# A two-layer hybrid transformer block: group C first in the mixer, and the projections of the conv, D and A beside later attention

## Chip, core and metric

One core of a Trainium2 chip. The metric is the device time of one execution in microseconds (us); the kernel before was executed three times, and once more with a profile.

## What is computed

The block has two layers. Each modulates and normalizes 512 latent tokens (and 256 context tokens) of width 1024, projects them once by `w_in` and cuts the result into four head groups. Cut to what the change touches:

```python
def hybrid_mixer(hx, hc, ...):
    qa, ka, va, ub, qc, kc, vc, qd, kd, vd = project(hx, w_in)        # and the same of hc
    y_a = window_gqa(qa, ka, va, ka_c, va_c, sink)                    # A: windowed attention
    y_b = conformer_conv(ub, conv_w, conv_b, conv_ln_g, conv_ln_b)    # B: 31 taps, depthwise
    y_c = diff_out(diff_attention_latent(qc, kc, vc, kc_c, vc_c, lam), subln_g, lambda_init)
    y_d = neighbourhood_attn(qd, kd, vd, kd_c, vd_c, rpb)             # D: 2-D windows
    return concatenate([y_a, y_b, y_c, y_d]) @ w_out                  # layer 0 also for the context
def diff_weights(q, k, v, lam):                                       # C: two softmaxes per head
    p = softmax(einsum(q, k) * C_QK_DIM ** -0.5)
    return einsum(p[:, :, 0] - lam * p[:, :, 1], v)
```

A gated residual, a SwiGLU network of hidden width 2816 and a second gated residual follow. The last layer drops the context's outputs.

## The kernel before

All tensors are kept in float32 accuracy: each weight and each activation is split into a high part and a low part (`split`, L138: a cast on ScalarE, then a subtraction, L143, on VectorE or GpSimd), and `mm3` (L173) multiplies high by high, high by low and low by high. A "unit" is 128 output columns of `w_in`: 24 matmuls of 512 latent columns, and 24 of 256 context columns where the context is needed, into a PSUM pair. It is loaded by SyncE's queue, split, multiplied and taken out of PSUM.

The mixer of a layer is written as Python generators, which `layer` (L985) interleaves: `beside` (L918) runs a main generator and advances a side one at a ratio, `mix2` (L937) alternates two, `take` and `chain` cut and join them. This written order is the input of a list scheduler with a timeline, which then fixes the order of the instructions of each engine; what an engine does at a given place is therefore read from the built order and not from the Python code.

Before, the mixer starts with three units of the conv (`first_units`, L441, with the columns `B0`, whose weights `ahead_b` asked for), which fill the time while the activations are still being normalized. `proj_b` (L568) makes the conv's gated input `hp` (L587) from two units for each half u. `conv_taps` (L862) is 29 multiply-adds (L873) on VectorE for each half, after the first tap on ScalarE (L870), and L877 for the last. `proj_c` (L552) makes q and k of a half of C and, for half 0, V. Then come `c_attn` (L632) for halves 0 and 1, `d_attn` (L772) for halves 0 and 1 and `a_attn` (L820), each beside projections of the next group: C's half 0 beside the rest of C's projections and D's half 0, C's half 1 beside the rest of D, D beside A. In C a step is a score of two softmaxes (L625), two maxima with the weighted copy out of PSUM (L656), exponentials on ScalarE, and one multiply-add on VectorE (L665), on which TensorE's transposes (L510) and the product with V (L616) wait. In D the score is L788, the maximum L799 and the division L816 on GpSimd. In A they are L625, L849 and L816; its context queries go through L729 to L743. The norms of C and of the conv (`c_norm`, L673, `conv_norm`, L881) stand beside D's half 1. `load_wo` (L947) splits the output projection's weights.

## Time and profile before

| | us |
|---|---|
| three executions | 1812.6, 1810.37, 1809.29 |
| median | 1810.37 |
| profiled execution | 1809.8 |
| span of its profile | 1808.0 |
| mixer of layer 0, start of the first units to w_out | 58 to 427 |
| mixer of layer 1 | 1085 to 1380 |

The profile is of one execution. A row of the page's first part gives an engine's busy time, its share of the span and its count of instructions. In a window's row the first number after the stretch is its length, then follow busy times by engine, the clock that TensorE was granted (1.00 is the full one) and the share and rate of the DMA. In a timeline's row the bracket at the end holds the engine's idle time ahead of the instruction and what ended it. Outside the two mixers TensorE has hardly any gap.

### The profile page before, as it was taken

How to read it: one execution, taken by the hardware profiler on the slowest of the kernel's cores; microseconds unless marked ns; L12 is line 12 of the kernel's file. 1: busy time of each engine (PE TensorE's matmuls, PEld its weight loads, DVE VectorE, ACT ScalarE, POOL GpSimd, SP SyncE). 2: the span in 40 equal slices, each digit the busy share in tenths (PEclk: the TensorE clock that was granted, in tenths of full speed). 3: DMA queues.
4: the chain of work that ended last, by engine and by line, in shares of the span. 5: the costliest groups of instructions: out<-in, count | busy, mean ns of one | idle time of the engine just before them, and what ended most of it. 6: DMA issues, size and time to landing. Idle time of an engine off the chain costs nothing.

```text
span 1808.0 us, 26990 instructions
## 1 busy us (share of the span) xinstructions
PE 1715.8 (95%) x11236; PEld 1415.6 (78%) x11236; DVE 941.5 (52%) x1546; ACT 586.3 (32%) x1052; POOL 216.8 (12%) x200
## 2 busy tenths in 40 slices
PE   6898999888999999999999999999988999999997
PEld 4786787666898878888888888878766888888886
DVE  5599656664362442332424347976565445444354
ACT  4223553553151112121120224345355332321322
POOL 1101202340000010000100011130342000000002
PEclk8998999898999999999999999999999999999999
DMA  9351102215134344234231221120225173323321
GB/s 322 89 155 36 45 24 78 82 38 201 60 93 143 121 140 130 83 96 131 62 107 43 83 81 59 49 66 25 89 61 175 36 209 93 105 83 92 117 70 47
DMA packets 187977, 172.79 MB, mean 96 GB/s; under 512 B 17878, under 2 KB 150478, under 8 KB 187726
## 3 DMA queue, kind: packets, MB, share of 16 engines
q1 hardware_dynamic: 187854, 171.06, 31.0%
q8 instruction: 88, 1.44, 0.3%
q14 instruction: 35, 0.29, 0.0%
HBM read 166.76 MB, written 4.52 MB: 95 GB/s over the span
## 4 chain that ended last, share of the span: by engine, by line
PE 81%; DVE 9%; DMA 4%; ACT 2%; issue 2%; POOL 1%; SPq 1%; POOLq 0%; ACTq 0%; DVEq 0%
PE ps L176 19%; PE ps L177 19%; PE ps L178 19%; PE pu L176 4%; PE pu L178 4%; PE pu L177 4%; DVE accd L873 3%; PE pt L616 2%; PE sc L625 2%; PE pt L510 2%; PE ada L306 2%; PE pu L616 1%; DVE Pm L656 1%; SPq L97 1%; DMA araw<-in_w_ada 1%
## 5 line engine op out<-in xcount | busy, mean ns | idle before, releaser
L177 PE MATMUL ps<-h,whi 128*128 128x512 f32 (+1 forms) x1104 | 383.5, 348 | 2.5 <-DVE h L143 2.5
L176 PE MATMUL ps<-h,whi 128*128 128x512 f32 (+1 forms) x1104 | 382.5, 349 | 0.9 <-DVE gt L974 0.9
L178 PE MATMUL ps<-h,wlo 128*128 128x512 f32 (+1 forms) x1104 | 382.9, 347 | 0.0
L141 ACT CAST whi<-wraw 128x1024 fp32r<-128x1024 f32 (+1 forms) x132 | 134.5, 1023 | 445.7 <-PE ps L177 246.8
L143 DVE TENSOR_TENSOR wlo<-wraw,whi 128x1024 fp32r<-128x1024 f32 (+1 forms) x116 | 140.1, 1211 | 199.0 <-ACT whi L141 198.0
L177 PEld LDWEIGHTS ps<-h,whi 128*128 128x128 f32 x1104 | 209.0, 189 | 29.8 <-DVE h L143 3.2
L176 PEld LDWEIGHTS ps<-h,whi 128*128 128x128 f32 x1104 | 207.8, 189 | 29.7 <-issue 2.8
L178 PEld LDWEIGHTS ps<-h,wlo 128*128 128x128 f32 x1104 | 208.8, 189 | 27.5 <-issue 2.0
L176 PE MATMUL ps<-wdhi,zh 128*128 128x512 f32 x440 | 171.7, 392 | 0.4 <-ACT ntmp L381 0.4
L177 PE MATMUL ps<-wdlo,zh 128*128 128x512 f32 x440 | 171.0, 390 | 0.0
L178 PE MATMUL ps<-wdhi,zl 128*128 128x512 f32 x440 | 170.5, 391 | 0.0
L176 PE MATMUL pu<-hT,whi 128*128 128x512 f32 (+1 forms) x456 | 163.2, 358 | 4.8 <-DVE hp L587 2.2
L177 PE MATMUL pu<-hT,whi 128*128 128x512 f32 (+1 forms) x456 | 160.7, 353 | 0.0
L178 PE MATMUL pu<-hT,wlo 128*128 128x512 f32 (+1 forms) x456 | 160.5, 352 | 0.0
L974 DVE TENSOR_TENSOR gt<-ps,g 128x1024 f32<-128x1024 f32 x66 | 80.6, 1222 | 142.7 <-PE ps L178 114.3
L141 ACT CAST wdhi<-wraw 128x1024 fp32r<-128x1024 f32 x44 | 46.1, 1052 | 271.3 <-PE ps L178 181.0
L977 POOL TENSOR_TENSOR x<-x,gt 128x1024 f32<-128x1024 f32 x12 | 29.7, 2474 | 729.8 <-DVE gt L974 729.8
L873 DVE SCALAR_TENSOR_TENSOR accd<-hp,wcol,accd 128x783 f32<-128x783 f32 (+1 forms) x116 | 112.8, 972 | 2.8 <-ACT accd L870 1.2
L1241 DVE TENSOR_TENSOR sg<-sg,ps 128x768 f32<-128x768 f32 (+1 forms) x44 | 36.1, 821 | 144.1 <-PE ps L178 116.1
L176 PEld LDWEIGHTS pu<-hT,whi 128*128 128x128 f32 x456 | 86.5, 190 | 21.0 <-issue 2.6
L176 PEld LDWEIGHTS ps<-wdhi,zh 128*128 128x128 f32 x440 | 82.6, 188 | 19.3 <-issue 1.4
L178 PEld LDWEIGHTS pu<-hT,wlo 128*128 128x128 f32 x456 | 86.8, 190 | 12.7 <-issue 1.8
(263 smaller groups left out, 2730.3 us busy)
## 6 DMA issues: line engine op xcount, KB each, us to landing
araw<-in_w_ada SPq DMA_DIRECT2D x60, 512.0 KB
wraw<-in_w_gate SPq DMA_DIRECT2D x44, 512.0 KB
wraw<-in_w_up SPq DMA_DIRECT2D x44, 512.0 KB
wraw<-in_w_down SPq DMA_DIRECT2D x44, 512.0 KB
wraw<-in_w_in SPq DMA_DIRECT2D x40, 512.0 KB
wraw<-in_w_ada SPq DMA_DIRECT2D x20, 512.0 KB
wraw<-in_w_out SPq DMA_DIRECT2D x12, 512.0 KB
whi<-in_w_ada SPq DMA_DIRECT2D x8, 512.0 KB
```

What stands on the lines that cost most here:

```text
L141: nc.scalar.copy(hi, src)
L143: eng.tensor_tensor(lo, src, f32(hi), op=ALU.subtract)
L176: mm(out, st[0], mv[0], start=first, stop=False)
L177: mm(out, st[0], mv[1], start=False, stop=False)
L178: mm(out, st[1], mv[0], start=False, stop=last)
L306: nc.tensor.matmul(ps[32 * j:32 * j + 32, 0:P], self.cstat[:, k, :], raw[:, a * 512 + j * P:a * 512 + (j + 1) * P], start=(k == 0), stop=( ...
L510: self.nc.tensor.transpose(pt[:, (i - a) * P:(i - a + 1) * P], blocks[i], self.ident)
L616: self.burst_of([lambda i=i, j=j: nc.tensor.matmul(po[64 * j:64 * j + 64, 0:P], *parts[j][i], start=(i == n - 1), stop=(i == 0)) for i in ...
L625: return [lambda o=o, q=q[a][r], k=k[b][r], i=i: self.nc.tensor.matmul(o, q, k, start=(i == 0), stop=(i == 2)) for i, (a, b) in enumerate( ...
L873: nc.vector.scalar_tensor_tensor(acc[:, 0:w], hp[:, k:k + w], wc, acc[:, 0:w], op0=ALU.mult, op1=ALU.add)
L974: nc.vector.tensor_tensor(tmp, ps, g, op=ALU.mult)
L1241: nc.vector.tensor_tensor(sg, sg, pss[1][:, 0:W], op=ALU.mult)
```

## The change

The first three units are now C's q and k of half 0 and one unit of the conv (`FIRST`); `first_units` takes a flag for the context for each unit, and `qk_unit` accepts a unit that is already in PSUM. After C's q and k and the conv's half 0 follow V, some taps and the modulation's loads. C's half 0 stands beside the conv's half 1 and the rest of C, C's half 1 beside D's half 0 and D's V, D's half 0 beside D's half 1 and C's norm, D's half 1 beside three units of A, and A beside A's last unit, the conv's norm, the loads of w_out and the modulation. The taps are given to C and D by `spread`. The conv's pool stays until A ends, and there are 9 buffers of the tag "qk" instead of 12. The diff, without the renaming of `ahead_b` and the changes of `first_units`:

```diff
...
-    QKB = 12
+    QKB = 9
...
-        lat, cx = self.unit(u, H, ctx, order)
+        lat, cx = u if len(u[0].shape) == 2 else self.unit(u, H, ctx, order)
...
-            self.qkc[nm, u] = self.qk_unit(self.w_unit(w, c0 + u * P), H, cx, sc, pool, (C_CC, C_SC, 1))
+            got = self.first.pop(c0 + u * P, None)
+            self.qkc[nm, u] = self.qk_unit(got or self.w_unit(w, c0 + u * P), H, cx, sc, pool, (C_CC, C_SC, 1))
...
-    B0 = (UB + 256, UB, UB + 256 + P)
+    FIRST = (CQ, CK, UB + 256)
...
+    def spread(self, main, side, nm, ns):
+
+        k = i = 0
+        for c in main:
+            i += 1
+            while k * nm < ns * i:
+                next(side, None)
+                k += 1
+            yield c
...
-        for u in range(2):
-            for _ in self.mix2(self.proj_b(l, H, c1, u), tp if u else iter(()), 3, False):
-                pass
+        self.half = 0
...
-        for _ in self.mix2(self.mix2(self.proj_c(l, H, c1, 0), tp, 6, False), adas, 2, False):
+        pc = self.proj_c(l, H, c1, 0)
+        for _ in self.mix2(self.take(pc, 2), self.proj_b(l, H, c1, 0), 1):
             pass
-        for _ in adas:
+        for _ in self.mix2(self.mix2(pc, tp, 5, False), adas, 4):
             pass
...
-        self.beside(self.mix2(self.c_attn(l, 0), tp, 1 + l, False),
-                    self.chain(self.proj_c(l, H, c1, 1), self.proj_d(l, H, c1, 0)), 2 * nq, 4)
-        self.beside(self.mix2(self.c_attn(l, 1), tp, 1 + l, False), d_rest(), 2 * nq, 4)
+        self.beside(self.spread(self.c_attn(l, 0), tp, 2 * nq, 14),
+                    self.chain(self.proj_b(l, H, c1, 1), self.proj_c(l, H, c1, 1)), 2 * nq, 4)
+        self.beside(self.spread(self.c_attn(l, 1), tp, 2 * nq, 16), self.chain(self.proj_d(l, H, c1, 0), d_v()), 2 * nq, 4)
         self.psum_pop()
         self.psum_push("e")
+        self.act_evac = False
         dn = 10 if cx else 8
         pa = self.proj_a(l, H, c1)
-        self.beside(self.d_attn(l, held["c2"], 0), self.take(pa, 3), dn, 3)
-        self.beside(self.d_attn(l, held["c2"], 1), rest(), dn, 14 if cx else 9)
+        self.beside(self.spread(self.d_attn(l, held["c2"], 0), tp, dn, 17),
+                    self.chain(self.proj_d(l, H, c1, 1), self.c_norm(l, c1)), dn, 5 if cx else 4)
+        for _ in tp:
+            pass
+        self.beside(self.d_attn(l, held["c2"], 1), self.take(pa, 3), dn, 3)
...
-        self.beside(self.chain(self.a_attn(l, 0), self.a_attn(l, 1)), more(), 2 * dn, 12)
+        self.beside(self.chain(self.a_attn(l, 0), self.a_attn(l, 1)), more(), 2 * dn, 21 if cx else 18)
         wop = held["wop"]
         held["c2"].release()
+        self.cv.release()
...
```

The built order, at the three places that the prediction speaks of. (The diff adds lines, so L656, L665, L873, L877 of before are L657, L666, L874, L878 of the change; `accd` is a tap's sum, `Pm` a softmax's weights, `sc` and `sd` the scores of C and D.)

First, VectorE at the end of layer 0's conv. Before, 30 taps stand ahead of C's first softmax and 28 behind it, and the last ones between the eighth step and the ninth:

```order
L656 ISA Pm_1694,nm_1693<-sc_1679,zcol_92 128x768
L656 ISA nm_1693 128x1
L656 ISA Pm_1698,nm_1697<-sc_1679,zcol_92 128x768
L656 ISA nm_1697 128x1
L873 SCALAR_TENSOR_TENSOR accd_1251<-hp_764,wcol_698,accd_1251 128x783
L143 TENSOR_TENSOR qk_1894<-pu_1895,qk_1893 128x512
L877 SCALAR_TENSOR_TENSOR yB_745<-hp_764,wcol_698,accd_1251 128x512
L877 SCALAR_TENSOR_TENSOR yB_745<-hp_764,wcol_698,accd_1251 128x256
```

With the change 19 stand ahead and 39 behind, and the last ones beside the tenth step, a narrow one of the context:

```order
L666 SCALAR_TENSOR_TENSOR Pm_1690<-Pm_1694,cf_1699,Pm_1690 128x256
L657 ISA Pm_1721,nm_1720<-sc_1708,zcol_92 128x256
L657 ISA nm_1720 128x1
L874 SCALAR_TENSOR_TENSOR accd_2011<-hp_1162,wcol_698,accd_2011 128x783
L663 RECIPROCAL rl_1724<-l_310_1715 128x1
L874 SCALAR_TENSOR_TENSOR accd_2011<-hp_1162,wcol_698,accd_2011 128x783
L665 SCALAR_TENSOR_TENSOR cf_1726<-L_184_1121,nlam_713,rl_1724 128x1
L874 SCALAR_TENSOR_TENSOR accd_2011<-hp_1162,wcol_698,accd_2011 128x783
L666 SCALAR_TENSOR_TENSOR Pm_1717<-Pm_1721,cf_1726,Pm_1717 128x256
L878 SCALAR_TENSOR_TENSOR yB_745<-hp_1162,wcol_698,accd_2011 128x512
L878 SCALAR_TENSOR_TENSOR yB_745<-hp_1162,wcol_698,accd_2011 128x256
```

So the conv ends two steps of C later than before, and ahead of D in both.

Second, TensorE in layer 0's D half 0, with the change: a piece of the run from one unit's last matmul (`pu`) to the next unit, over seven D scores (L789 and L626, of six rows each, two shown):

```order
L178 MATMUL pu_2828<-hT_71_342,wlo_2822 128x256
L510 MATMUL ptd_2771<-ident_88,Pm_2762 128x128 x4
L789 MATMUL sd_2907<-qk_2112,qk_1917 128x256 x2
L789 MATMUL sd_2907<-qk_2113,qk_1917 128x256 x2
...
L685 MATMUL pu_2937<-ident_88,yC_746 128x128 x4
...
L510 MATMUL ptd_2811<-ident_88,Pm_2802 128x128 x4
L789 MATMUL sd_2985<-qk_2112,qk_1917 128x256 x2
```

Between these scores only transposes and products with V stand (L510, L617, L685); four units of A follow in one piece. Before, the units stand between D's scores up to the seventh, and none behind it.

Third, VectorE at the end of layer 0's A. Before, two splits of w_out and three of the next weights (two are in this piece) stand among the rows of the last context softmax (L729 to L743):

```order
L732 TENSOR_SCALAR nm_943_4520<-nm_943_4520,sink_714 128x2
L143 TENSOR_TENSOR wolo_971_4611<-wraw_4608,wohi_970_4610 128x1024
L734 TENSOR_SCALAR es_945_4524<-nm_943_4520,sink_714 128x2
L143 TENSOR_TENSOR wlo_4626<-wraw_4623,whi_4625 128x1024
L524 COPY PT_4486<-pt_4490 128x512
L729 TENSOR_REDUCE nm_949_4541<-sc_4506 128x2
L740 TENSOR_TENSOR ls_944_4522<-ls_944_4522,es_945_4524 128x2
L143 TENSOR_TENSOR wlo_4632<-wraw_4629,whi_4631 128x1024
```

With the change they stand behind it, and six earlier ones at the start of A, which were in D before:

```order
L143 TENSOR_TENSOR wolo_860_4172<-wraw_4168,wohi_859_4171 128x1024
L901 TENSOR_SCALAR qk_3775<-pu_3765,bmv_3770,brs_3772 128x256
L143 TENSOR_TENSOR wolo_869_4195<-wraw_4191,wohi_868_4194 128x1024
L850 ISA Pm_3676,nm_3678<-sc_3663,mask_3657,sink_714 128x512
...
L744 TENSOR_SCALAR Pm_4539<-Pm_4539,ls_950_4542 128x256 x2
L524 COPY PT_4496<-pt_4497 128x512
L143 TENSOR_TENSOR wolo_968_4605<-wraw_4602,wohi_967_4604 128x1024
L143 TENSOR_TENSOR wolo_971_4611<-wraw_4608,wohi_970_4610 128x1024
```

So A's last softmax has no split ahead of it, and A's first (L850) has two.

## Rows read from the trace of the kernel before

**Rows 1.** The page: busy time, share of the span and instructions of TensorE.

```profile
PE 1715.8 (95%) x11236; PEld 1415.6 (78%) x11236; DVE 941.5 (52%) x1546; ACT 586.3 (32%) x1052; POOL 216.8 (12%) x200
```

**Rows 2.** Windows of layer 0: length, busy (instructions) per engine, granted clock, DMA.

```profile
72.00:126.00 54.00, 50.94 (x428) 43.95 (x428) 45.34 (x55) 11.46 (x17) 1.95 (x1) 1.00 0.48 139
126.00:187.00 61.00, 53.24 (x321) 42.41 (x321) 59.16 (x87) 23.86 (x47) 10.33 (x4) 0.89 0.16 45
...
206.50:284.00 77.50, 75.44 (x556) 60.04 (x554) 44.19 (x113) 38.36 (x94) 4.76 (x2) 1.00 0.14 36
...
328.70:358.30 29.60, 22.34 (x181) 16.56 (x180) 21.50 (x51) 19.31 (x43) 12.04 (x9) 0.83 0.40 125
358.30:386.00 27.70, 19.03 (x162) 14.30 (x162) 20.97 (x70) 16.78 (x45) 13.05 (x15) 0.88 0.00 1
...
407.00:427.00 20.00, 12.48 (x102) 8.95 (x103) 11.95 (x25) 11.91 (x33) 2.04 (x2) 0.75 0.51 162
```

**Rows 3.** Windows of layer 1, same columns.

```profile
1148.00:1207.00 59.00, 55.99 (x340) 43.29 (x339) 56.06 (x92) 28.40 (x56) 19.97 (x17) 0.97 0.25 67
...
1267.00:1324.00 57.00, 53.48 (x433) 41.44 (x432) 32.73 (x79) 23.46 (x58) 23.58 (x29) 1.00 0.22 71
1324.00:1380.50 56.50, 45.91 (x509) 34.83 (x507) 35.59 (x103) 34.85 (x78) 21.98 (x22) 0.94 0.30 87
```

**Rows 4.** Timeline at 167 us: start, length, engine, line [idle before <-releaser].

```profile
167.50 3.09 DVE L665 SCALAR_TENSOR_TENSOR Pm<-Pm,cf,Pm 128x768 f32<-128x768 f32 x1
...
170.74 1.51 PE L510 MATMUL pt<-ident,Pm 128*128 128x128 f32 x6 [4.72 <-DVE Pm L665]
```

**Rows 5.** Timeline in D's end, TensorE.

```profile
336.50 0.66 PE L510 MATMUL ptd<-ident,Pm 128*128 128x128 f32 x4 [2.64 <-POOL Pm L816]
```

**Rows 6.** Timeline at A's end, VectorE: one of five weight splits.

```profile
412.34 1.21 DVE L143 TENSOR_TENSOR wolo<-wraw,wohi 128x1024 fp32r<-128x1024 f32 x1
```

**Rows 7.** Timeline at A's end, TensorE.

```profile
419.21 1.09 PE L510 MATMUL pt<-ident,Pm 128*128 128x128 f32 x4 [2.65 <-DVE Pm L743]
```

**Rows 8.** Timeline, TensorE: C's first and twelfth score, D's first.

```profile
125.79 0.97 PE L625 MATMUL sc<-qk,qk 32*128 32x512 f32 x6
...
208.96 0.63 PE L625 MATMUL sc<-qk,qk 32*128 32x256 f32 x6
...
284.14 0.98 PE L788 MATMUL sd<-qk,qk 64*128 64x256 f32 x12 [0.35 <-DVE nm L656]
```

**Rows 9.** Timeline, TensorE: first and last of a unit's 48 matmuls.

```profile
94.96 0.50 PE L176 MATMUL pu<-hT,whi 128*128 128x512 f32 x1
...
103.37 0.28 PE L178 MATMUL pu<-hT,wlo 128*128 128x256 f32 x1
```

**Rows 10.** Groups of VectorE in layer 0's mixer: busy us, mean ns of one.

```profile
L873 DVE SCALAR_TENSOR_TENSOR accd<-hp,wcol,accd 128x783 f32<-128x783 f32 x58 | 63.9, 1102 | 1.8 <-ACT accd L870 1.2
L656 DVE CUSTOM_DVE_ANT_0 Pm<-sc,zcol 128x768 f32<-128x768 f32 x32 | 29.3, 952 | 15.2 <-PE sc L625 15.1
L665 DVE SCALAR_TENSOR_TENSOR Pm<-Pm,cf,Pm 128x768 f32<-128x768 f32 x16 | 18.3, 1145 | 0.3
```

**Rows 11.** Timeline, VectorE: the conv's last operations, layer 0.

```profile
191.34 1.14 DVE L877 SCALAR_TENSOR_TENSOR yB<-hp,wcol,accd 128x512 f32<-128x512 f32 x2
```

**Rows 12.** Timeline, VectorE: taps while GpSimd splits a weight.

```profile
130.66 3.01 DVE L873 SCALAR_TENSOR_TENSOR accd<-hp,wcol,accd 128x783 f32<-128x783 f32 x2
...
137.86 2.55 DVE L873 SCALAR_TENSOR_TENSOR accd<-hp,wcol,accd 128x783 f32<-128x783 f32 x1
```

**Rows 13.** Groups of GpSimd in layer 0's mixer.

```profile
L816 POOL TENSOR_TENSOR Pm<-Pm,r 128x512 f32<-128x512 f32 x24 | 25.5, 1074 | 94.8 <-DVE r L815 93.7 <-PE pt L616 0.8 <-PE pu L178 0.3
L143 POOL TENSOR_TENSOR wlo<-wraw,whi 128x1024 fp32r<-128x1024 f32 x8 | 19.8, 2481 | 148.6 <-ACT whi L141 148.6
```

**Rows 14.** Timeline, TensorE: C's first score in layer 1.

```profile
1147.95 1.32 PE L625 MATMUL sc<-qk,qk 32*128 32x512 f32 x12
```

**Rows 15.** Groups of VectorE in layer 1's mixer.

```profile
L873 DVE SCALAR_TENSOR_TENSOR accd<-hp,wcol,accd 128x512 f32<-128x512 f32 x58 | 48.9, 843 | 1.0
```

More of the change, by code (lines that the diff above doesn't have):

```diff
@@ L447, in first_units @@
                 a = two[n]
-                outs.append((a[:, 0:512], a[:, 512:768] if nctx else None))
+                outs.append((a[:, 0:512], a[:, 512:768] if nctx[n] else None))
             else:
-                outs.append((self.ps("pu"), self.ps("pu")[:, 0:256] if nctx else None))
-        groups = [(0, 0, 256), (0, 256, 512)] if not by_k else [(0, 0, 512)]
-        if nctx:
-            groups.insert(0, (1, CTX0, CTX0 + 256))
-        for g in [groups] if by_k else [[g] for g in groups]:
-            self.abreast(ws, [[o[1] if x else o[0][:, a:b] for x, a, b in g] for o in outs], H, g, by_k)
+                outs.append((self.ps("pu"), self.ps("pu")[:, 0:256] if nctx[n] else None))
+        cgr = (1, CTX0, CTX0 + 256)
+        for g in [[cgr, (0, 0, 512)]] if by_k else [[(0, 0, 256)], [(0, 256, 512)], [cgr]]:
+            on = [n for n in range(len(c0s)) if nctx[n] or not g[0][0]]
+            self.abreast([ws[n] for n in on], [[outs[n][1] if x else outs[n][0][:, a:b] for x, a, b in g] for n in on],
+                         H, g, by_k)
             if between:
@@ L560, in proj_c, with ahead_first @@
             yield from self.v_units(w, CV, H, self.v_to(self.VC))
-    def ahead_b(self, l):
-        for c0 in self.B0:
+    def ahead_first(self, l):
+        for c0 in self.FIRST:
             self.ahead(self.t["w_in"][l], c0)
-    B0 = (UB + 256, UB, UB + 256 + P)
+    FIRST = (CQ, CK, UB + 256)
     def proj_b(self, l, H, pool, u):
@@ L1007, in layer @@
             next(adas)
-            self.ahead_b(0)
+            self.ahead_first(0)
             for _ in adas:
@@ L1047, in layer @@
         self.psum_push("c")
-        self.first_units(l, H, self.B0, cx, l == 0,
+        self.first_units(l, H, self.FIRST, (cx, True, cx), l == 0,
                          l and (lambda: self.norm_pair(1, 0, self.rows, order[0], H, npool, "pt")))
@@ L1071, in layer, with d_v @@
         tp = taps()
-        for u in range(2):
-            for _ in self.mix2(self.proj_b(l, H, c1, u), tp if u else iter(()), 3, False):
-                pass
+        self.half = 0
         self.burst, self.ada_tag, self.atags = 0, "pt", [("wraw", 3, F32, self.wst)]
         adas = self.ada_gen([(0, 3)] if l == 0 else [])
-        for _ in self.mix2(self.mix2(self.proj_c(l, H, c1, 0), tp, 6, False), adas, 2, False):
+        pc = self.proj_c(l, H, c1, 0)
+        for _ in self.mix2(self.take(pc, 2), self.proj_b(l, H, c1, 0), 1):
             pass
-        for _ in adas:
+        for _ in self.mix2(self.mix2(pc, tp, 5, False), adas, 4):
             pass
-        held = {}
         wo, wa = [], (6, 2)[l]
         nq = 6 if cx else 4
-        def d_rest():
-            yield from self.proj_d(l, H, c1, 1)
-            for _ in tp:
-                pass
-            self.cv.release()
-            self.act_evac = False
+        held = {}
+        def d_v():
             c2 = held["c2"] = self.pool("mixd", "left")
@@ L1098, in d_rest, with more @@
                 yield
-        def rest():
+        def more():
             yield from pa
-            self.half = 0
             hTp.release()
             held["wop"] = self.pool("wo", "right")
-            self.maska = self.tl(held["c2"], [P, 768], "mask")
-            self.dma(self.maska[:, 0:640], t["maska"])
-            yield from self.c_norm(l, c1)
             yield from self.conv_norm(l, c1)
-        def more():
             self.burst, self.ada_tag = 15, ("pu", "pt")[l]
@@ L1257, in layer @@
                     pass
-                self.ahead_b(1)
+                self.ahead_first(1)
                 h2p.release()
```

3 lines of the change are left out of this document (2 added, 1 removed).

## The prediction, made before the changed kernel ran

> **What bounds the kernel now.** I read the engine table first: PE is busy 1715.8 of 1808.0 us [rows 1]. Almost all the time is matmul work that the change leaves as it is; what can be won or lost is PE's lost time, which is its idle time and its busy time at a lowered clock. The windows show where that lies [rows 2]. For a window, loss = length − PE busy + (1 − clock) × length; the last term because a granted clock of 0.89 means that 22% of the window ran at half speed (1.2 instead of 2.4 GHz), which costs 11% of it. In layer 0 that gives 3.1 us in 72:126, 14.5 in 126:187 (7.8 idle, 6.7 clock), 2.1 in 206.5:284, 12.3 in 328.7:358.3 (7.3 and 5.0), 12.0 in 358.3:386 and 12.5 in 407:427: 56.5 us. In layer 1 it is 4.8 in 1148:1207, 3.5 in 1267:1324 and 14.0 in 1324:1380.5: 22.3 us [rows 3]. So the change could win at most about 79 us.
>
> Next I asked what ends the losses. In 126:187 DVE is busy 59.16 of 61.0 us [rows 2]: PE waits for DVE there, which has the conv's taps and C's softmax in one queue. The longest gap is 4.72 us, ended by the DVE multiply L665 [rows 4]. In D's end (328.7:358.3) no projection is left to fill PE while it waits for the softmax and for L816 on POOL: one gap is 2.64 us [rows 5]. At the end of A the context softmax stands behind weight splits in DVE's queue [rows 6], and PE waits 2.65 us for L743 [rows 7].
>
> **The change, part by part.** The arithmetic stays the same and only its order changes, so I price each stage by what PE loses in it.
>
> *From the start to C's twelfth score.* The first C score stands at 125.79 us [rows 8]. A unit of 768 columns takes 48 matmuls, the first at 94.96 and the last at 103.37 us: 8.4 us [rows 9], which is 24 of 512 columns at 0.233 and 24 of 256 at 0.117. In the built order six units' worth of matmuls (50.4 us at these prices) stand ahead of the first score where eight stood (67.2). So the score comes 16.8 us earlier, and of the 3.1 us lost ahead of it I take 2 as saved: 107 us.
>
> From there DVE is the limit, and it has more to do than before. 39 of the 58 taps now stand behind the first score on DVE, where 28 did; 19 stand ahead of it, where 30 did. All 58 end before C's eleventh step: none goes to D, whatever the new call of `spread` says. Up to the end of the conv DVE does 39 taps at 1.10 us (43.0), 16 wide L656 at 0.95 (15.2), 8 wide L665 at 1.145 (9.2) [rows 10], and some 63 small operations (narrow steps, reads, factors, two weight splits, rope), which I estimate from the same rows by their widths at 19 in all. Sum 86: the conv would end at 193. The means hold contention with POOL's weight splits already; if four of those cost DVE their share once more (below), it is 199. Before, the conv ended at 192.4 [rows 11], with two units more done. I put the twelfth score at 198 instead of 208.96 [rows 8]; but 16.8 us of projection that were done by then are still to do: 198 + 16.8 = 214.8, some 6 us behind (1 to 10). Part of the gaps takes rope transposes that stood later, so I take **+5**. The cover that kept DVE's taps cheap was PE's own work ahead of C; it is gone, and what is late next is PE itself, behind L666.
>
> A split on POOL lasts 2.48 us [rows 13]. Beside one, a tap took 2.55 (1.10 is the mean of all), two taps 3.01 (for 2.2), an L665 3.09 (for 1.145) [rows 4, 12]: 1.4 us lost on DVE in the mean. The Trainium skill (SBUF — State Buffer, section "SBUF: two separate sides") has a rule that speaks against this change: GpSimd and a DVE operation with two SBUF inputs take a shared port pair by an exclusive lock, and the loser is blocked for the whole of the other's instruction. By that rule a DVE queue packed with taps would pay up to 2.5 for each of some six splits, 6 us more than by the rows, and the sum below would be +9 instead of +3.
>
> *C's second half, up to D's first score*, is bounded by PE: 77.5 us with 2.1 lost [rows 2]. The matmuls between the two scores are the same within about 1 us. **0.**
>
> *D.* Before, 19.6 us of projection (built order, at the prices above) stood in D, and its last 29.6 us had none; now 37.3 us stand in it. But they stand in two pieces: the built order has a run of seven D scores without a unit, then four units. Each of the seven groups needs two L816 on POOL at 1.07 us [rows 13], so 2.1, and on PE a score of 0.98 [rows 8] with transposes and value products of about twice that, so 3: PE can go on if the scores run ahead. The six w_out splits that DVE did in this window (1.21 each [rows 6]) have left D. I take a loss of 7 where 12.3 were, between 4 (a third of it, as if only the half of the idle time stayed) and 9 (seven groups at the old window's share). **−5.**
>
> *A.* It has no unit beside its attention, as before. At its end the last context softmax has no weight split ahead of it on DVE any more: the gap of 2.65 us [rows 7] and most of the lowered clock behind it go, 5 to 8 of the 12.5 lost there. But the six w_out splits (7.3 us on DVE) and the rope of A's last unit now stand among A's first softmaxes, where PE lost 12.0 already, and the conv's norm is there too. They cost between 0 (if DVE's gaps take them) and 10; I take 5. **−1.5**, from −8 to +5.
>
> *Layer 1.* Its unit is 5.6 us (24 × 0.233), so the first C score, at 1147.95 before [rows 14], comes 11 us earlier, at 1137. Then 38 taps stand behind it instead of 27: 38 at 0.84 (32.0 [rows 15]) and seven softmaxes at 3.6 (25, by rows 10 two L656, one L665 and 0.5 of small ones) put DVE's part of the eighth step at 1194 or later; I put that score, at 1207 before, at 1197. By then 14.2 us of projection are still to do that were done before: 4 us behind, and a bit of clock, **+5** (0 to 8). D: seven score groups with less beside them than before, **+2.5**; A: the units that end later cover D's end instead, **−2.6**.
>
> *Edits that cost nothing.* D's bias tiles are built early on POOL, while the first units run; were they to hold the split queued behind them, a unit would wait once, no longer than two splits (5 us). Two more splits of each layer go to POOL and leave DVE. Nine qk buffers instead of twelve hold what lives together in this order; if one is short, one C step waits. The FFN is untouched.
>
> The sum: 5 + 0 − 5 − 1.5 + 5 + 2.5 − 2.6 = +3.4 us. The profiled execution took 1809.8 us, 0.6 under the median of 1810.37, so 1813.2 on the one scale and 1813.8 on the other: I say **1813**. A measurement of this kernel can tell about 0.2%, 3.6 us, from no change; the forecast is inside that.
>
> **The rivals.**
> *Faster: the cover works.* C's scores run far enough ahead of DVE, and PE has units of B, C and D to do meanwhile. C's first stage then loses half of what it did: −7. D loses 2, as its covered part did: −10. A loses 6 less at its end and pays nothing at its start: −6. Layer 1 as forecast: +5. That is −18, 1792. For it: every one of these gaps has its cause in the rows, and the last cause is surely removed. Against: DVE was busy 97% of 126:187 [rows 2] and gets 11 taps more. Chance 0.30.
> *Slower: DVE stays the bound for the whole of C's first half.* PE idles 20 us there and twice falls to the lower clock (4 each): 28 lost where 17.6 were, +10. Layer 1 does the same, +8. In A the six splits hold the first softmaxes and the clock falls once more, +5 after its end's gain. D wins 5. That is +18, 1828. It decides from the point where the conv ends after about 203 us. For it: DVE's 86 us are a sum without a single gap. Chance 0.25.
> *The change does what its words say*, and the taps go on into D. The built order excludes it; DVE would end C's first half some 15 us earlier and the first rival would hold, which its chance includes.
>
> **How the numbers follow.** The forecast has 0.45 (1806 to 1820): of it 0.06 lies below 1806.8, 0.22 within 3.6 us of no change, 0.17 above. With the rivals: faster 0.36, same 0.22, slower 0.42. The range for 8 in 10 reaches into both rivals: 1794 to 1829.
>
> **What would show it.** C's first score at 105 to 109; the end of the conv (L878) at 193 to 199, with DVE over 95% busy between them and PE losing 20 to 24 us; D's first score near 270 instead of 284.14; 4 to 9 us lost in D; A's first score within 4 us of 358; the gap behind L744 at A's end gone, and new gaps behind L850 at its start. A conv that ends before 188, or an A that loses under 18, would make the forecast wrong on the fast side; a conv that ends after 203 on the slow one.

## The result, and the profile after

| | before | with the change |
|---|---|---|
| runs (us) | 1812.6, 1810.37, 1809.29, 1811.31 | 1825.97, 1821.45, 1825.4, 1826.75 |
| median (us) | 1810.84 | 1825.68 |
| ratio, 95% interval | | 1.0077 (1.0059 to 1.0096) |
| span of the profile (us) | 1808.0 | 1824.0 |

The change makes the kernel 0.8% slower, some 14 us by the ratio. The engine row of the page says that TensorE does the same work, 4.5 us more of busy time in 16 us more of span:

```profile
PE 1720.3 (94%) x11236; PEld 1419.1 (78%) x11236; DVE 942.5 (52%) x1537; ACT 584.0 (32%) x1057; POOL 230.4 (13%) x204
```

The places of the loss follow from the starts of the first instruction of each stage in both traces. A stage that is longer because it holds more projection is not slower, so its projection is counted by the prices of the prediction (0.233 and 0.117 us a matmul).

| stage | us before | us after | projection moved out (−) or in (+) | lost (+) or won (−) |
|---|---|---|---|---|
| layer 0, first units to D's first score (from 58) | 226.1 | 217.9 | −17.7 | +9.4 |
| D of layer 0 | 74.1 | 84.5 | +17.7 | −7.3 |
| A of layer 0 | 68.6 | 62.9 | 0 | −5.7 |
| w_out and FFN of layer 0 | 663.9 | 666.5 | 0 | +2.6 |
| layer 1, first units to D's first score | 176.1 | 185.7 | −8.0 | +17.6 |
| D of layer 1 | 57.6 | 64.6 | +8.0 | −0.9 |
| A of layer 1 | 56.1 | 56.1 | 0 | 0 |
| rest | 427.5 | 427.9 | 0 | +0.4 |

The last column sums to 16 us, the difference of the spans. So C's stage lost 27 us in both layers together, D and A won 14, and 2.6 were lost behind A. The windows of layer 0 (columns as in [rows 2], which they answer to):

```profile
96.00:103.20 7.20, 0.24 (x3) 0.03 (x1) 1.27 (x2) 0.00 (x0) 0.00 (x0) 0.79 0.54 152
...
140.00:170.00 30.00, 29.30 (x220) 24.81 (x221) 28.99 (x47) 12.65 (x26) 5.07 (x2) 1.00 0.12 36
170.00:187.90 17.90, 16.16 (x111) 13.14 (x109) 17.83 (x26) 7.39 (x18) 2.50 (x1) 0.90 0.11 30
187.90:204.00 16.10, 9.03 (x66) 5.98 (x66) 16.07 (x34) 8.13 (x25) 2.36 (x1) 0.79 0.11 33
...
275.90:312.00 36.10, 31.30 (x298) 24.53 (x298) 28.36 (x76) 19.39 (x54) 21.95 (x27) 1.00 0.04 11
312.00:347.00 35.00, 34.15 (x234) 28.29 (x232) 10.40 (x22) 7.48 (x19) 4.76 (x5) 1.00 0.21 62
...
360.30:386.00 25.70, 17.77 (x143) 12.98 (x141) 23.19 (x62) 15.88 (x35) 12.50 (x12) 0.80 0.48 143
...
407.00:423.20 16.20, 11.99 (x197) 8.68 (x196) 7.54 (x21) 8.27 (x23) 0.00 (x0) 0.93 0.55 152
```

And of layer 1, to be read beside [rows 3]:

```profile
1137.80:1155.80 18.00, 18.00 (x93) 13.99 (x92) 17.82 (x27) 8.19 (x14) 2.65 (x1) 1.00 0.31 88
1155.80:1176.40 20.60, 16.33 (x99) 12.55 (x98) 20.49 (x33) 8.66 (x17) 5.25 (x2) 0.92 0.18 52
1176.40:1200.00 23.60, 18.31 (x127) 13.65 (x126) 23.46 (x36) 9.20 (x19) 5.19 (x2) 0.91 0.16 45
1200.00:1223.60 23.60, 23.02 (x121) 18.54 (x121) 13.29 (x24) 8.78 (x21) 2.40 (x1) 0.80 0.08 23
...
1275.40:1340.00 64.60, 62.32 (x481) 49.24 (x480) 36.88 (x95) 23.48 (x60) 25.72 (x32) 1.00 0.20 63
1340.00:1396.10 56.10, 42.97 (x476) 32.87 (x474) 38.59 (x97) 34.42 (x74) 20.70 (x19) 0.86 0.32 96
```

DVE is busy 17.82 of 18.0, 20.49 of 20.6 and 23.46 of 23.6 us from C's first score of layer 1 on, and TensorE loses 4.3 and 5.3 us of idle time in the second and third of these windows and, with clocks of 0.92, 0.91 and 0.80, 8.5 more in the second to the fourth. Before, that stretch lost 4.8 [rows 3]. In D's window of layer 0 (275.9 to 312) 4.8 us are idle at the full clock, where the uncovered end of D lost 12.3 before [rows 2].

Timeline rows of TensorE, in order: the wait ahead of the first C score, that score, the longest wait in C, C's twelfth score, D's first, the wait ahead of w_out, and two waits in layer 1's C (they answer to [rows 4, 7, 8]); one wait at A's start stands ahead of w_out's:

```profile
103.20 1.08 PE L306 MATMUL pt<-wraw,cstat 128*32 128x128 f32 x16 [6.97 <-DMA wraw<-in_w_ada]
...
116.44 0.73 PE L626 MATMUL sc<-qk,qk 32*128 32x512 f32 x4
...
195.87 1.51 PE L510 MATMUL pt<-ident,Pm 128*128 128x128 f32 x6 [4.68 <-DVE cf L665]
...
203.91 0.39 PE L626 MATMUL sc<-qk,qk 32*128 32x256 f32 x2
...
275.86 0.97 PE L789 MATMUL sd<-qk,qk 64*128 64x256 f32 x12
...
364.84 1.14 PE L626 MATMUL sc<-qk,qk 64*128 64x384 f32 x12 [3.14 <-DVE nm L850]
...
423.22 0.80 PE L176 MATMUL ps<-wohi,yh 128*128 128x512 f32 x1 [3.87 <-ACT yh L141]
...
1171.50 0.68 PE L510 MATMUL pt<-ident,Pm 128*128 128x128 f32 x4 [2.41 <-DVE Pm L666]
...
1197.48 0.87 PE L510 MATMUL pt<-ident,Pm 128*128 128x128 f32 x3 [3.27 <-DVE Pm L666]
```

The conv of layer 0 ends at 203.0 (201.88 and 1.14), where it ended at 192.5 before [rows 11]:

```profile
201.88 1.14 DVE L878 SCALAR_TENSOR_TENSOR yB<-hp,wcol,accd 128x512 f32<-128x512 f32 x2
```

The first wait is not in the prediction: 6.97 us for weights of the modulation, ahead of a first C score at 116.44. SyncE's queue shows why:

```profile
84.68 14.21 SPq L97 DMA_DIRECT2D dB<-rpt  x21
98.99 1.41 SPq L97 DMA_DIRECT2D wraw<-in_w_ada  x3
```

21 of the small loads of D's bias (`dB`, 8 per head) stand in the queue for 14.2 us, and the three loads that TensorE waits for stand behind them. The issue of one takes 0.43 us (median of the layer's 32). Of the rest, 3.3 us are waits until GpSimd, which builds the bias tiles from two buffers, is done with one of them. The queue's own waits between 74 and 104 us have the row (total, times, longest):

```profile
SPq L97 <- POOL dnb L770: 3.3, 2, 2.8
```

Before, the bias tiles lay in memory that came free only when the conv's pool was released, and their loads stood behind the conv's end:

```profile
192.90 7.54 SPq L97 DMA_DIRECT2D dB<-rpt  x16
```

Now that pool stays and D's tiles lie on top of it, so the loads are ready from the start and the scheduler puts them first.

### The profile page after: what moved, and what is told of

Same layout as the page of the kernel before. It is cut to its first block, busy times and chain, and to the rows that moved or that the text cites. A ratio compares the mean times of both kernels' runs of the same rounds, so it can differ in the third digit from the quotient of the medians.

```text
span 1824.0 us, 26992 instructions
## 1 busy us (share of the span) xinstructions
PE 1720.3 (94%) x11236; PEld 1419.1 (78%) x11236; DVE 942.5 (52%) x1537; ACT 584.0 (32%) x1057; POOL 230.4 (13%) x204
## 4 chain that ended last, share of the span: by engine, by line
PE 76%; DVE 11%; DMA 4%; ACT 3%; SPq 2%; issue 2%; POOL 2%; POOLq 0%; ACTq 0%; DVEq 0%
PE ps L176 19%; PE ps L178 18%; PE ps L177 18%; DVE accd L874 4%; PE pu L176 3%; PE pu L178 3%; PE pu L177 3%; SPq L97 2%; PE pt L510 2%; PE sc L626 2%; PE ada L306 2%; PE pt L617 2%; DVE Pm L657 1%; DVE Pm L666 1%; DMA wraw<-in_w_out 1%
## 5 line engine op out<-in xcount | busy, mean ns | idle before, releaser
L874 DVE SCALAR_TENSOR_TENSOR accd<-hp,wcol,accd 128x783 f32<-128x783 f32 (+1 forms) x116 | 112.0, 966 | 3.7 <-ACT accd L871 2.1
L1246 DVE TENSOR_TENSOR sg<-sg,ps 128x768 f32<-128x768 f32 (+1 forms) x44 | 36.1, 821 | 143.9 <-PE ps L178 115.5
L510 PE MATMUL pt<-ident,Pm 128*128 128x128 f32 x432 | 73.5, 293 | 27.3 <-DVE Pm L666 10.2
```

What stands on the lines that cost most here:

```text
L510: self.nc.tensor.transpose(pt[:, (i - a) * P:(i - a + 1) * P], blocks[i], self.ident)
L874: nc.vector.scalar_tensor_tensor(acc[:, 0:w], hp[:, k:k + w], wc, acc[:, 0:w], op0=ALU.mult, op1=ALU.add)
```

## The experiments

Times are medians of 4 to 12 executions and are compared as ratios to the kernel before, executed in turn with them (1808.6 to 1809.9 us in the four sets); the changed kernel at 1.0077 stands at 1822.5 to 1823.8 on those scales. Stages are read from one profile of each kernel. Executions of one kernel differ by up to 8 us, so a microsecond or two of a stage says little. Most edits also make the scheduler build a new order around them.

**Late bias loads.** `behind` adds an order of issue between two instructions of one engine and no wait.

```diff
+        self.anchor = self.last_dma if u == 0 else None
         nbs = [self.d_bias(l, 2 * u + j, pool) for j in range(2)]
...
-            self.dma(B[r * 16:(r + 1) * 16], self.rpt[a:a + 8].rearrange("k c w -> c k w"))
+            self.behind(self.dma(B[r * 16:(r + 1) * 16], self.rpt[a:a + 8].rearrange("k c w -> c k w")), self.anchor)
```

> Edit: the changed kernel, but D's 32 bias loads of each layer are queued on SyncE behind the last weight load written ahead of them, instead of wherever the scheduler puts them. Nothing else is ordered. Theory 1 (in layer 1 DVE is saturated by taps pulled ahead of the softmax, which costs some 17 us; in layer 0 a queue of bias loads on SyncE costs 8.5 us: 7.0 idle and 1.5 of clock): the gap of 6.97 us in layer 0 goes, C's first score comes at 107 to 110 instead of 116.4; part of it is lost again behind DVE, so the whole gains 3 to 8 us over the changed kernel (1818 to 1823); layer 1's C stage is as before within 2 us. Rival 2 (the early bias work on SyncE and GpSimd is the cause of the loss in both layers): 12 to 17 us gained, 1809 to 1814. Rival 3 (DVE's work decides layer 0's first stage whatever the start): no gain in time, the wait moves behind DVE, 1824 to 1827.

Measured: 1816.53 us, ratio 1.0041 (1.0029 to 1.0054), 6 us under the changed kernel. TensorE's timeline has the first C score at 106.99, where the prediction had it, and D's first score 8.4 us earlier than the change:

```profile
106.99 1.20 PE L631 MATMUL sc<-qk,qk 32*128 32x512 f32 x10
...
267.46 0.97 PE L795 MATMUL sd<-qk,qk 64*128 64x256 f32 x12
```

and the conv's end at 194.6 (193.45 and 1.14), near the 193 of the prediction's sum:

```profile
193.45 1.14 DVE L884 SCALAR_TENSOR_TENSOR yB<-hp,wcol,accd 128x512 f32<-128x512 f32 x2
```

Layer 1 hardly moves (units to D's first score 184.9 instead of 185.7). TensorE, VectorE and ScalarE have all their instructions in the same order in both kernels, so only the loads and GpSimd's bias tiles stand elsewhere. So the bias queue costs 8.4 us in layer 0 by these two profiles (the whole gains 6 by the medians), as Theory 1 said, and is not the cause in layer 1: the second rival falls.

**Taps held to where the code has them.** Each tap is ordered on DVE behind the last softmax operation ahead of it in the code.

```diff
-                nc.vector.scalar_tensor_tensor(acc[:, 0:w], hp[:, k:k + w], wc, acc[:, 0:w], op0=ALU.mult, op1=ALU.add)
+                self.behind(nc.vector.scalar_tensor_tensor(acc[:, 0:w], hp[:, k:k + w], wc, acc[:, 0:w], op0=ALU.mult,
+                                                           op1=ALU.add), self.comb)
```

> Edit: the changed kernel, but each tap is ordered on DVE behind the softmax operation of C or D that is written ahead of it (order only, no wait on another engine), so that the taps are really spread over C and the first half of D. Theory 1 (taps pulled ahead saturate DVE in C): layer 1's C stage loses under 6 us instead of 18.6, TensorE's waits for L666 of 1.7, 2.4, 1.0 and 3.3 us shrink under 1 us each, D gets slower by 2 to 5 us; in layer 0 the 4.7 us wait at 195.9 goes too. Gain over the changed kernel 10 to 20 us: 1806 to 1816. Rival 2 (bias work early): under 3 us of gain. Rival 4 (too little projection stands in C, so that TensorE runs out of work and the taps are only the nearest thing it waits for): C's waits move to other rows, D is slower by what the taps cost there, and the whole is 1822 to 1832.

> Edit: both edits of the two other runs. Theory 1: the gains add, less 0 to 3 us, since with the taps held back DVE has room when C begins earlier: 15 to 26 us under the changed kernel, 1800 to 1811, the same as the kernel before or a little faster. Rival 2: no faster than with the bias loads alone. Rival 4: no faster than with the bias loads alone, 1818 to 1826.

Measured: 1832.69 us, ratio 1.0134 (1.0118 to 1.015), and with the late bias loads 1825.01, 1.0087 (1.0074 to 1.0101). Both are slower than without the held taps, by some 10 and 8 us, so the sum that I expected fell, and the totals are near those of Rival 4 (1822 to 1832, and 1818 to 1826). Half of the theory held, though. In layer 1 the stretch from the first units to D's first score (1099.31 to 1272.12) takes 172.8 us instead of 185.7, and the waits for the multiply L666 are gone from it, all but one of 3.2 us for a maximum; with the bias loads late as well it is 174.9. But D takes 76.6 instead of 64.6 us in layer 1 and 97.0 instead of 84.5 in layer 0. Rows of TensorE, one in layer 0's D, D's first score of layer 1 and one in its D:

```profile
301.49 2.16 PE L516 MATMUL ptd<-ident,Pm 128*128 128x128 f32 x8 [5.62 <-POOL Pm L823]
...
1272.12 0.98 PE L795 MATMUL sd<-qk,qk 64*128 64x256 f32 x12
...
1299.50 1.76 PE L623 MATMUL pt<-PT,VD 128*64 128x128 f32 x13 [2.37 <-DVE PT L530]
```

In layer 1 the longest waits in D are for DVE's evacuations, which stand among taps (up to 2.37 us). In layer 0 the longest, 5.62 us, is for a division on GpSimd, whose sums DVE had ready at 294.5; from 292.3 to 300.3 GpSimd built the bias tiles of D's half 1, which came ahead of the division in this order. So the 12 us of layer 0's D are not the taps' alone. What the change's words promise, taps in the first half of D, is worth 13 us in layer 1's C and costs 12 in its D: seven D scores stand there with little projection beside them.

**Weight splits on DVE.** All splits that stand on GpSimd are done on DVE, in the changed kernel, in the one with late bias loads, and in the kernel before.

```diff
-            eng = nc.gpsimd if pool else nc.vector
+            eng = nc.vector
```

> Edit: the changed kernel, but the 20 weight splits that stand on GpSimd are done on DVE. Theory 1: each gives DVE 1.2 us of work in place of the 1.4 us that it loses beside GpSimd's 2.5, and TensorE no longer waits for a split of 2.5: within 4 us of the changed kernel, 1821 to 1829. Rival 5 (the contention of DVE with GpSimd's splits is what makes DVE the limit): 6 to 14 us faster, 1811 to 1819.

> Edit: the late bias loads and all weight splits on DVE, both on the changed kernel. If the two gains are of different places (8.5 us of SyncE's queue in layer 0; DVE blocked beside GpSimd's splits in C, mostly in layer 1): they add, 1816.5 and 1817.8 against 1822.5 make 1811 to 1813. If they are the same wait seen twice: 1815 to 1817.

> Edit: the kernel before with its 16 weight splits of GpSimd on DVE. If the contention hurts wherever DVE is dense with taps, the kernel before gains too, since its layer 0 has four splits in the stretch where DVE is busy 97%: 3 to 7 us faster than before. If the gain is special to the changed kernel, where the splits meet taps that TensorE is waiting for: within 3 us of before.

Measured: the changed kernel 1817.79 us, 1.0051 (1.0038 to 1.0065), some 5 us faster, a gain between the two expectations; with late bias loads 1814.71, 1.0029 (1.0018 to 1.0039), where adding would have given 1.0015 and the same wait twice 1.0041, so that this one settles nothing; the kernel before 1799.61, 0.9942 (0.9929 to 0.9954), 10 us faster than itself, more than I thought possible. DVE gets 20 more splits to do in the changed kernel and 16 in the kernel before, and TensorE waits less for it. Its busy time does not grow all the same. The engine row of the kernel before with its splits on DVE, to be read beside [rows 1] (941.5):

```profile
PE 1716.7 (95%) x11236; PEld 1416.8 (79%) x11236; DVE 938.7 (52%) x1562; ACT 587.2 (33%) x1052; POOL 177.2 (10%) x184
```

Sixteen splits at 1.21 [rows 6] are 19.4 us more, and the sum is 2.8 less: DVE's other operations became some 22 us shorter, 1.4 us for each split. In the changed kernel (942.4 after 942.5, with 20 splits more) it is 1.2. Groups of VectorE in layer 1's mixer, first of the changed kernel:

```profile
L874 DVE SCALAR_TENSOR_TENSOR accd<-hp,wcol,accd 128x512 f32<-128x512 f32 x58 | 49.1, 847 | 1.8 <-ACT accd L871 0.9
...
L666 DVE SCALAR_TENSOR_TENSOR Pm<-Pm,cf,Pm 128x768 f32<-128x768 f32 x16 | 18.4, 1147 | 0.3
```

and of the kernel before with its splits on DVE:

```profile
L873 DVE SCALAR_TENSOR_TENSOR accd<-hp,wcol,accd 128x512 f32<-128x512 f32 x58 | 43.3, 747 | 2.4 <-ACT accd L870 1.9
...
L665 DVE SCALAR_TENSOR_TENSOR Pm<-Pm,cf,Pm 128x768 f32<-128x768 f32 x16 | 16.2, 1015 | 0.3
```

A tap falls from 0.847 us (0.843 before, [rows 15]) to 0.747, a wide multiply from 1.147 to 1.015. How it happens is seen in one pair of the changed kernel, GpSimd's row and then DVE's:

```profile
1194.05 2.47 POOL L143 TENSOR_TENSOR wlo<-wraw,whi 128x1024 fp32r<-128x1024 f32 x1 [8.23 <-ACT whi L141]
```

```profile
1193.58 0.74 DVE L874 SCALAR_TENSOR_TENSOR accd<-hp,wcol,accd 128x512 f32<-128x512 f32 x1
1194.24 3.09 DVE L666 SCALAR_TENSOR_TENSOR Pm<-Pm,cf,Pm 128x768 f32<-128x768 f32 x1
```

The split runs from 1194.05 to 1196.52. The multiply that begins at 1194.24 takes 3.09 us and ends 0.81 behind the split's end, and TensorE's wait of 3.27 us at 1197.48 ends with it. The Trainium skill (SBUF — State Buffer, section "SBUF: two separate sides") states that a DVE operation with two SBUF inputs and a GpSimd operation that reads SBUF take the shared port in turn, and that the later one is blocked until the other is done; this pair agrees. The mean of 1.4 us that the prediction took from its rows is right for the whole kernel, but the price is uneven: this multiply alone lost 2.1 us (3.09 against 1.015), and that falls on TensorE when it waits for that multiply.

Two things limit the reading. The order changed with the edit: in layer 1 of the kernel before, C's first score now stands 45.9 us behind the first unit instead of 57.2, and 41 taps begin behind it instead of 29, so the 10 us are the contention and the new order together. And the splits cost the kernel before no less than the changed one: with the splits on DVE in both, the change is 1.0051 / 0.9942, 1.1% slower, where it was 0.8%. So GpSimd's splits are a cost of both kernels, and not what makes the change slower.

**Start undone.** The first units and the conv's two halves as before; D's projections and A's units beside later attention, as in the change; bias loads late.

```diff
-    FIRST = (CQ, CK, UB + 256)
+    FIRST = (UB + 256, UB, UB + 256 + P)
...
-                    self.chain(self.proj_b(l, H, c1, 1), self.proj_c(l, H, c1, 1)), 2 * nq, 4)
+                    self.proj_c(l, H, c1, 1), 2 * nq, 2)
```

> Edit: the changed kernel with its start undone: the first three units and the conv's two halves come first, as before, with 3 and 6 taps a step beside them, and C's half 0 stands beside C's half 1 alone. What comes after (D's projections and A's units beside later attention, the conv's norm in A) stays as in the change, and D's bias loads are queued late. If the start (taps that begin later while C begins earlier) is what costs: C's stage in layer 1 loses under 6 us again as before, and the whole is as before or faster by what A's end and D gain, 1800 to 1810 on the scale where before is 1808.6. If the later half (D and A) costs instead: 1814 to 1822, no faster than the run with the late bias loads (1816.5).

Measured: 1824.89 us, ratio 1.0082 (1.0069 to 1.0094). Slower than both things expected, and 7 us slower than the change's start with the late bias loads (1.0041). In this kernel C's half 0 has two units beside it instead of four, and none from its sixth score to its twelfth in layer 0; in layer 0 TensorE is idle for 12.9 us in the window of half 0, where 7.8 were before [rows 2], and in layer 1 at the end of half 0, with a lower clock behind it:

```profile
125.60:187.00 61.40, 48.54 (x324) 39.67 (x324) 61.02 (x89) 25.59 (x51) 19.14 (x14) 0.90 0.21 54
...
1175.00:1200.00 25.00, 20.17 (x121) 14.37 (x121) 24.81 (x40) 11.28 (x24) 5.75 (x2) 0.92 0.16 45
1200.00:1225.00 25.00, 20.52 (x152) 16.84 (x149) 15.65 (x35) 14.20 (x31) 2.40 (x1) 0.81 0.00 1
```

DVE is full in the first two of these windows (61.02 of 61.4, 24.81 of 25.0) and TensorE waits for it; in the third DVE has room and the clock is at 0.81. With the projection counted, the stage up to D's first score loses 12.0 us in layer 0 and 10.8 in layer 1. The start is not what costs; C's half 0 is slow with 29 taps, as many as before, when the projections beside it have been sent to later groups.

**Taps in C's half 1.** The held taps with other numbers: 18 beside half 0, 29 beside half 1, none in D; bias loads late. And the same with the splits on DVE.

```diff
-        self.beside(self.spread(self.c_attn(l, 0), tp, 2 * nq, 14),
+        self.beside(self.spread(self.c_attn(l, 0), tp, 2 * nq, 18),
...
-        self.beside(self.spread(self.c_attn(l, 1), tp, 2 * nq, 16), self.chain(self.proj_d(l, H, c1, 0), d_v()), 2 * nq, 4)
+        self.beside(self.spread(self.c_attn(l, 1), tp, 2 * nq, 29), self.chain(self.proj_d(l, H, c1, 0), d_v()), 2 * nq, 4)
```

> Edit: the changed kernel with late bias loads and the taps ordered behind the softmax steps, but 18 beside C's half 0, 29 beside C's half 1 and none in D (DVE was busy 15 of 28 us in C's half 1). If taps cost only where DVE is short (C's half 0, and D with its chains over GpSimd): C's half 0 gains what the spread run gained (10 to 13 us in layer 1, 5 in layer 0) and D loses nothing: 1800 to 1808 on the scale where before is 1808.6 and the run with late bias loads alone 1816.5. If taps cost wherever they stand beside attention: 1813 to 1822.

> Edit: the changed kernel with the late bias loads, the taps held to 18 beside C's half 0 and 29 beside C's half 1, and all weight splits on DVE. If taps that crowd C's half 0 and GpSimd's splits beside them are two causes that add: the run with the held taps (1.0005 of before) gains another 2 to 6 us, ratio 0.997 to 0.9995. If with held taps the splits no longer meet a tap that TensorE waits for: ratio 1.000 to 1.003, since DVE's own split work then only adds.

Measured: 1810.81 us, ratio 1.0005 (0.9996 to 1.0014), 6 us faster than with late bias loads alone and equal to before; with the splits on DVE 1811.66, 1.0012 (1.0002 to 1.0023), no faster. In layer 1 the stretch to D's first score takes 171.2 us instead of 184.9, as much as the fully spread taps won, and its windows show why (from C's first score to D's first):

```profile
1134.40:1155.00 20.60, 20.60 (x114) 16.33 (x114) 16.52 (x26) 11.59 (x19) 5.04 (x2) 1.00 0.30 88
1155.00:1175.00 20.00, 20.00 (x134) 16.13 (x132) 13.38 (x26) 9.30 (x19) 10.56 (x12) 1.00 0.33 69
1175.00:1196.00 21.00, 18.09 (x129) 13.91 (x129) 17.96 (x31) 11.06 (x24) 3.02 (x2) 0.92 0.17 50
1196.00:1220.00 24.00, 24.00 (x170) 19.77 (x169) 18.96 (x34) 12.34 (x27) 4.01 (x2) 1.00 0.08 23
1220.00:1257.40 37.40, 37.03 (x284) 30.29 (x282) 31.73 (x60) 20.52 (x45) 3.17 (x2) 1.00 0.15 43
```

DVE has room in all of them, and TensorE is idle for 3.3 us and loses one drop of the clock. Of the taps 16 begin in half 0 here; with late bias loads alone it is 42, and in the kernel before 29. D takes 68.2 us there (64.6 with late bias loads alone), and in layer 0 D takes 87.8 (84.4) and A 64.7 (61.9), while C won only 1.3: so D lost where none was expected, and the total came out between the two expectations. In layer 0 D's idle time is as without the edit (4.5 us of its first 36, 4.8 there), but its clock is 0.91 instead of 1.00, which makes 3.2 us; what brought the clock down is not shown. The last run says that, with the taps held, taking the splits from GpSimd wins nothing more: in its profile layer 1's stage takes 177.9 us, 7 more than with them on GpSimd.

**The kernel before with the same two edits.** Splits on DVE, taps ordered behind the softmax steps that its own code has ahead of them.

> Edit: the kernel before with all weight splits on DVE and its taps ordered behind the softmax steps that stand ahead of them in the code, so that some 28 taps behind C's first score spread over both halves of C instead of crowding half 0 (the start, the units and the later groups stay as before). If crowding in half 0 is a cost of its own also there: 3 to 8 us faster than the kernel before with the splits on DVE (0.9942), ratio 0.990 to 0.9925. If the contention with GpSimd was all that made DVE the limit before: within 2 us of 0.9942.

Measured: 1795.06 us, ratio 0.9919 (0.9903 to 0.9935), 4 us faster than with the splits alone (0.9942; the two intervals overlap). The window that lost 14.5 us before [rows 2] lost 2.7 with the splits alone, and now loses nothing:

```profile
126.00:187.00 61.00, 58.31 (x392) 47.20 (x391) 60.91 (x98) 29.27 (x58) 0.00 (x0) 1.00 0.17 51
...
126.00:187.00 61.00, 61.00 (x425) 49.22 (x424) 52.08 (x95) 32.24 (x66) 0.00 (x0) 1.00 0.19 55
```

**The start alone.** C first as in the change, but C's half 0 has the conv's half 1, C's half 1 and D's half 0 beside it, and everything behind it stands as before; then the same with the splits on DVE.

```diff
-                    self.chain(self.proj_b(l, H, c1, 1), self.proj_c(l, H, c1, 1)), 2 * nq, 4)
+                    self.chain(self.proj_b(l, H, c1, 1), self.proj_c(l, H, c1, 1), self.proj_d(l, H, c1, 0)), 2 * nq, 6)
...
+        self.beside(self.mix2(self.c_attn(l, 1), tp, 1 + l, False), d_rest(), 2 * nq, 4)
...
+        self.beside(self.d_attn(l, held["c2"], 0), self.take(pa, 3), dn, 3)
+        self.beside(self.d_attn(l, held["c2"], 1), rest(), dn, 14 if cx else 9)
```

> Edit: the change's start alone. C's q and k and one conv unit come first, the conv's half 1, C's half 1 and D's half 0 stand beside C's half 0, and everything behind that (D's half 1 and D's V beside C's half 1, A's units beside D, the norms in D, w_out's weights, 12 qk buffers, the bias loads behind the conv) stands as in the kernel before. If what costs in the change is work taken away from C's half 0 (too little projection beside a DVE that is full): with D's half 0 beside it again, C's stage of layer 1 comes within 5 us of before, and the whole is within 6 us of before, 1804 to 1815, ratio 0.997 to 1.003. If taps that start later are the cost by themselves: C's half 0 is as slow as in the run with late bias loads and now holds more, ratio 1.004 to 1.010.

> Edit: the same start alone, with all weight splits on DVE, to be compared with the kernel before with its splits on DVE (0.9942). If the start is neutral once the contention is gone: ratio 0.992 to 0.997. If taps behind C's first score cost by themselves (39 of them instead of 28): ratio 0.998 to 1.004. If an earlier C is a gain by itself: under 0.992.

Measured: 1810.01 us, ratio 1.0001 (0.9991 to 1.0011), the same as before; and 1791.83, 0.9905 (0.989 to 0.9919), the lowest median of this study, 17 us under the kernel before and 31 under the change (its interval overlaps that of the kernel before with both edits). In layer 1, to D's first score, the start alone takes 182.0 us with 1.9 us of projection less than before: 7.8 lost where the change lost 17.6, more than the 5 expected of that stage though the whole is as expected, since A of layer 1 gives 5.0 back and layer 0 some 2.5. With the splits on DVE it takes 172.5 with no projection less, 3.6 won. The window of layer 0 shows what is left of the loss of 14.5 us when DVE is full but not blocked:

```profile
126.00:187.00 61.00, 60.19 (x426) 48.91 (x426) 60.93 (x108) 29.84 (x65) 0.00 (x0) 1.00 0.12 35
```

DVE is busy 60.93 of 61.0 us and TensorE loses 0.8. So a full DVE need not hold TensorE up, but it can. Two windows of layer 1's C say when, both with no split on GpSimd, first of the start alone, then of the change:

```profile
1160.00:1193.00 33.00, 33.00 (x221) 26.02 (x221) 32.97 (x60) 18.23 (x36) 0.00 (x0) 1.00 0.17 49
```

```profile
1180.00:1200.00 20.00, 16.21 (x119) 11.53 (x118) 19.96 (x39) 9.91 (x22) 0.00 (x0) 0.91 0.18 52
```

DVE is full in both, with 43 taps behind C's first score. With the start alone, which has 8.8 us more of projection between C's first score and D's, TensorE loses nothing; in the change it is idle for 3.8 us, and the clock falls.

**The runs read together.** Layer 1 from the first units to D's first score, us lost (+) or won (−) against the kernel before, projection counted:

| | splits on GpSimd | splits on DVE |
|---|---|---|
| kernel before | 0 | −5.3 |
| start alone | +7.8 | −3.6 |
| the change | +17.6 | +8.3 |

Down a column, the change loses 9.8 and 11.9 more than the start alone: that is what its later groups cost. (Late bias loads change its two entries to 16.8 and 11.3, which shows how far single profiles of near kernels differ.) Across a row, the splits cost every one of the three kernels, the change 4 us more than the kernel before. The whole times say the same: 1.0041 with late bias loads, 1.0001 with the later groups as before as well. The start alone also has its taps given out by `mix2` instead of `spread`, 12 buffers and another order of D's parts, so that the missing projection is the likely and not the only possible part of it.

## Why the prediction was right, and where it was off

It forecast slower as the likeliest, 1813 within 1794 to 1829; the measured 1825.7 lies inside, near the slower rival's 1828. That says little for its sum: the range is 35 us wide and reaches into both rivals, and +3.4 stands against 14 to 16 measured. C's two terms were 17 us short, D and A came out 7 better than forecast, and 3 us behind A were in no term; that part of the errors cancelled is luck. By its steps:

- *C's first score of layer 0 at 107*: it came at 116.44. The step that failed is "edits that cost nothing": D's bias tiles were priced on GpSimd's queue, at most 5 us for a split behind them. No split waited there; their loads stood on SyncE's queue, 21 of them for 14.2 us ahead of weights that TensorE needed, and the prediction has nothing on SyncE's queue. With them late the score is at 106.99 and the conv's end at 194.6, against 107 and 193 of the sum; from the score to the conv's end it is 87.6 us (86.6 in the change itself), against 86. The wait makes up 8.4 of the 9.4 us lost in that stage; with late bias loads the stage loses 1.0 (217.9 − 8.4 = 209.5, and 17.7 of projection, against 226.1), where +5 was forecast.
- *D, −5*: it won 7.3 in layer 0. The run of seven scores without a unit kept TensorE busy 31.3 of 36.1 us at the full clock. Mechanism right, and inside the range of 4 to 9 us lost.
- *A, −1.5 (−8 to +5)*: it won 5.7 in layer 0. As forecast the wait for the last context softmax went and a new one came behind L850 (3.1 us at 364.84). What was not forecast is the wait of 3.87 us ahead of w_out (423.22, counted in A) and the clock of 0.75 in the 9.2 us behind it, 2.3 of the 2.6 us of the next row of the table. Its window:

```profile
423.20:432.40 9.20, 9.18 (x30) 7.07 (x31) 5.71 (x11) 4.00 (x9) 0.00 (x0) 0.75 1.02 370
```

- *Layer 1, C +5 (0 to 8)*: it lost 17.6. This is the term that makes up most of the error. Its mechanism was the right one in part, a DVE that is full with 38 taps behind C's first softmax; it was sized as DVE's work against the clock, as if the projection that leaves C's half 0 only had to be done later. The start alone has as many taps behind C's first score (42 of layer 1's 58 begin behind it in both traces) and loses 9.8 less, so work missing beside C's half 0 is the likely larger part. Moving the taps out of half 0 helps too: with 26 fewer there 13.7 us are won, but that is also 13 fewer than before, so it does not price the 11 that the change added. With the splits on DVE the change takes 175.7 us there against 185.7, with 0.7 of projection less; but the kernel before wins 5.3 by that edit. Each of the three edits gives back half or more, so the gains do not divide the loss among causes.
- *D and A of layer 1, +2.5 and −2.6*: −0.9 and 0. The −2.6 had no row behind it.
- The rule of the Trainium skill on the shared port was given as 6 us more, +9 instead of +3. The trace agrees that an operation is blocked for the rest of a split, and DVE's busy time agrees with the prediction's mean of 1.4 us for each. The gains of 5 and 10 us when the splits go to DVE hold a new order too, so they price neither; that the measured +14 is nearer to +9 than to +3 is no support for +9.
- The slower rival was priced at +10 and +8 for C in the two layers and named DVE as the bound. Layer 0's 9.4 is near its first number, but 8.4 of it came from SyncE's queue; layer 1's 17.6 is twice its second. The conv's end in layer 0, 203 us, stood at the point that it named only because C began 9.4 us late. That 1828 is near the measured time is luck too.

What stays open: the run with both the late bias loads and the splits on DVE does not tell whether those gains add; no run separates the clock's share from the waits ahead of it; no run puts only the projection back beside C's half 0; and no run changes the engine of a split, or the place of a tap, with all other instructions left in their order.

## What to carry to other kernels

A loop that hides dependent work needs its cover in the half that is short of it: count the independent TensorE work and the DVE work beside each stage, not over the whole. When a pool's memory becomes free earlier, look for loads that the scheduler will now pull ahead, and read the DMA queue's order as well as the compute engines'. Work given to GpSimd to relieve a full DVE can cost DVE as much as it takes over, when both read SBUF with two inputs: here DVE's busy time was no lower for it, and the kernel before was 10 us of 1810 faster without it, in a new order. A cost that both kernels have is no reason for the difference between them: apply the edit to both before calling it the cause.

## What was not expected of the hardware

- The contention was known from single rows; its sum was not. Sixteen splits of 2.5 us on GpSimd took some 22 us of DVE's time in the kernel before, more than the 1.2 us each that DVE needs to do them itself; with them on DVE that kernel is 10 us faster (0.9942).
- DVE at 99.9% of a stretch of 61 us (60.93) left TensorE idle for only 0.8 us of it with no split on GpSimd and enough projection beside it; in the kernel before with the same splits on DVE (60.91) it was 2.7.
- Small loads have a price in the queue that issues them: 21 loads held it 14.2 us, 0.43 us for the issue of one (median) and the rest in waits, 3.3 us of them for GpSimd to free a buffer.
